# First weights in smaller pieces, x first on its queue, and the last output block in two halves

## The chip, the cores and the metric

The kernel runs on one core of one Trainium2 chip. The metric is the device time of one execution in microseconds (us); the time before is the median of three runs.

## The reference

One decoder block on x of 1024 tokens by 1024 channels, in float32:

```
xn   = rms_norm(x, norm1_g);  proj = xn @ w_in          # 1024 -> 5632 columns, cut into nine parts
q, k = rms_norm per head of 64;  v
A[t,s] = sigmoid(z_ts) * prod_{s<j<t} (1 - sigmoid(z_tj));  o_sb = A v      # 8 heads, strictly causal
HGRN2: f = lb + (1-lb) sigmoid(f_in);  S_t = diag(f_t) S_{t-1} + (1-f_t) i_t^T;  o_t = S_t^T silu(q_t)   # 4 heads
o_hg = rms_norm(o) * silu(g)
h    = x + (sigmoid(gate_sb) * (o_sb @ Wb1) + sigmoid(gate_hg) * (o_hg @ Wb2)) @ w_out
out  = h + (silu(rms_norm(h) @ w_gate) * (rms_norm(h) @ w_up)) @ w_down     # hidden 2816
```

## The kernel before

**Layout.** Everything is held transposed: channels on the 128 partitions, tokens along the free dimension, in two halves h of 512 tokens. A float32 product is made of three matmuls: every operand is split into a high part in the type fp32r and a low part (the operand less its high part, again fp32r), and high*high, high*low and low*high are summed in one PSUM bank of 128x512.

**Stage 1** multiplies x by the 44 column tiles of w_in (each 1024x128, brought in as a 128x1024 tile). `take_x(h)` (L528) loads the eight 128x512 blocks of x of a half, makes `ah` (xh: x times norm1_g, on ACT) and `al` (xl: the rest, on DVE), and squares each block on ACT for the norm; DVE adds the squares up in `tail`, one matmul sums them over the channels, and ACT turns the result into the factor `rr` (Ln, then Exp). The products are made from x without this factor; it is multiplied in by DVE when a bank is read (`aa<-pj,rr`, L587 on). `proj(ws, h)` (L565) makes the 24 matmuls of one column tile and one half of the tokens, k = 0 to 7 with three matmuls each; the first call makes the first two column tiles (q and k of the first pair of heads) side by side, 48 matmuls. Three PSUM banks of the name `pj` take these products, so that a fourth product waits until DVE has read one of the first three.

**The first loads.** The gains vector `vt` (128x27) is loaded first on SP's DMA queue (L236). The first half (k = 0 to 3) of the first two weight tiles, 128x512 or 256 KB each, is loaded on ACT's queue (L343 to L347); their second halves and x come on SP's queue in the order that `load` chains: x0, x1, x2, the second half of tile 0, x3, the second half of tile 1, x4 and so on. The first halves are split by ACT (the cast, `oh<-kb`) and DVE (the subtraction, `ol<-kb,oh`), the second halves by POOL and DVE (`split_w`, L517), as are all later weights of the stage. A short setup on DVE and ACT (L291 to L305) makes small vectors out of `vt`. Before its first product PE makes nine matmuls on a constant (`WARM`, L364).

**The order.** Stage 1 to the gate and up projections is written as a list of operations with costs, priorities (`rank`; higher goes first, equal ranks by the longest way to the stage's end) and buffer rings. `Plan.issue` (L131) runs this list through a model of the engines and issues the instructions in the order found there, all from L194. A buffer of a ring is free again for the planner when every operation that reads, writes or `holds` it is done. The order is fixed before the run: each engine executes its instructions in it and waits where an input is late.

**The end.** The down projection multiplies 512-column blocks p = 0 to 10; the last product keeps the last three p (`LAST`) for the end: for each of its four row blocks d it makes 9 matmuls of 512 columns into one PSUM bank (L1152), DVE adds the bank to `hb` (L1160), and SP's queue stores 256 KB to the output (L1162).

Of the kernel before, what the change touches and what calls it, by code (L numbers as in the profile page):

```python
# [10 lines left out]
F32 = mybir.dt.float32  # L11
# [4 lines left out]
ALU = mybir.AluOpType  # L16
# [12 lines left out]
LEVELS = [64, 32, 16, 8, 4, 2, 1]  # L29
FILL = ["GgGGaifq", "gGaGfiqGG", "gaGGGiqGfGG", "gGGG"]  # L30
BANKS = [3, 2, 3]
WARM = 9
ORDER = [1, 6, 2, 5, 7, 4, 3]
DOWN = [1, 6, 2, 7, 5, 4, 3]

# [179 lines left out]
def hybrid_block(ctx: ExitStack, tc, xT, wi, wb, wo, wg, wu, wd, vec, outT):  # L215
# [17 lines left out]
        return bank("ms", BANKS[2])  # L233

    vt = const.tile([P, V_W], F32, name="vt")
    nc.sync.dma_start(vt, vec)  # L236

    def load_w(src, pool=None):
        t = (pool or wpool).tile([P, 1024], F32, tag="w", bufs=2, name="w32")
# [70 lines left out]
    def hs(h):  # L310
        return slice(h * HALF, (h + 1) * HALF)
# [28 lines left out]
    st1 = ExitStack()  # L340
    hgp = st1.enter_context(tc.tile_pool(name="hgp", bufs=1, reuse_waits="tile"))

    first_w = []  # L343
    for n, v in fill_cols[:2]:
        t = hgp.tile([P, HALF], F32, tag="kb", bufs=4, name="kb")
        nc.scalar.dma_start(t, wi[COL[n] + v][:, :HALF])
        first_w.append(t)  # L347
    nc.scalar.preload_act_table_set("natural_log_exp_and_others")
    pre = ExitStack()
    pp = pre.enter_context(tc.tile_pool(name="prep", bufs=1))  # L350
# [78 lines left out]
    def new(ring, shape=(P, HALF), dt=F32):  # L429
        pool, cap, tag, phase = where[ring]  # L430
        plan.ring(ring, cap)

        def make():
            open_pools(phase)
            return (pools[pool] if phase else pool).tile(list(shape), dt, tag=tag, bufs=cap, name=tag)

        return Buf(ring, make, phase)
# [8 lines left out]
    def V(fn, *args, n=HALF, aps=0, rank=0, part=False, holds=(), after=(), **kw):  # L446
        cycles = 2 * n if fn == nc.vector.tensor_tensor_scan else n
        us = 0.067 + cycles / 960 + 0.061 * aps
        return plan.op("V", us, [(fn, args, kw)], rank, after, part=part, holds=holds)
# [37 lines left out]
    def pool_copy(dst, src, rank=0, after=(), holds=()):  # L487
        return G(nc.gpsimd.tensor_scalar, dst, src, 1.0, 0.0, op0=ALU.mult, op1=ALU.add, us=0.68,
                 rank=rank, after=after, holds=holds)
# [24 lines left out]
    def load(dst, src, kb, rank=1):  # L514
        last_load[0] = L(dst, src, kb, rank=rank, after=(last_load[0],))

    def split_w(src):  # L517
        hi, lo = new("oh", dt=F32R), new("ol", dt=F32R)
        last_split[0] = pool_copy(hi, src, rank=1, after=(last_split[0],))
        V(tt, lo, src, hi.bitcast(F32), op=ALU.subtract, rank=1)  # L520
        return hi, lo

    def take_w(col):
        w = new("w", (P, 1024))
        load(w, wi[col], 512)
        return [split_w(w[:, 512 * i:512 * i + 512]) for i in range(2)]

    def take_x(h):  # L528
        ss, acc, ws, sqs = new("ms"), new("tail"), [[], []], []
        if h == 0:  # L530
            plan.ring("kb", 4)
            for u in range(2):
                w = Buf("kb", lambda u=u: first_w[u])
                hi, lo = new("oh", dt=F32R), new("ol", dt=F32R)
                plan.at[A(nc.scalar.copy, hi, w, rank=3)] = 2.4 + 0.6 * u
                V(tt, lo, w, hi.bitcast(F32), op=ALU.subtract, rank=2)
                ws[u].append((hi, lo))
        for k in range(KT):
            x = new("aa" if h == 0 else ("xf", "xq", "xi", "xg")[k // 2])
            load(x, xT[k][:, hs(h)], 256)  # L540
            if h == 0 and k in (2, 3):
                u = k - 2
                n, v = fill[u]
                w = new("kb")
                load(w, wi[COL[n] + v][:, HALF:], 256)
                ws[u].append(split_w(w))
            g = vt[:, V_N1 + k:V_N1 + k + 1]
            A(act, xh[k][h][:, hs(h)], x, AF.Copy, scale=g, aps=1, rank=2 - h)
            V(stt, xl[k][h][:, hs(h)], x, g, xh[k][h][:, hs(h)].bitcast(F32), op0=ALU.mult,
              op1=ALU.subtract, aps=1, rank=2 - h)  # L550
            if k == 0:
                A(act, acc, x, AF.Square, rank=1 - h)
            else:
                sq = new("ww")
                A(act, sq, x, AF.Square, rank=1 - h)
                sqs.append(sq)
        for sq in sqs:
            V(tt, acc, acc, sq, op=ALU.add, rank=1 - h)
        M(2048, [(ss, ones, acc, True, True)])
        rstd(rr[h], ss, D, rank=1 - h)  # L560
        return ws
# [3 lines left out]
    def proj(ws, h, after=None):  # L565

        pss = [new("pj") for _ in ws]
        for k in range(KT):
            cols = slice(k % 4 * P, (k % 4 + 1) * P)
            for ps, w in zip(pss, ws):  # L570
                hi, lo = w[k // 4]
                last_fill[0] = M(1536, [
                    (ps, hi[:, cols], xh[k][h][:, hs(h)], k == 0, False),
                    (ps, hi[:, cols], xl[k][h][:, hs(h)], False, False),
                    (ps, lo[:, cols], xh[k][h][:, hs(h)], False, k == KT - 1)],
                    rank=-1, after=(last_fill[0], after))
            after = None
        return pss

# [600 lines left out]
            for d in range(4):  # L1180
                finish(o, d)
    rest = [(p, operands(o, p)) for p in range(NP - LAST, NP)]
    for d in range(4):
        for p, ops in rest:
            step(o, d, p, ops, False)
        finish(o, d)


def _layout(inputs):
# [45 lines left out]
```

## Time and profile before

| | us |
|---|---|
| median of 3 runs (lowest to highest) | 1520.84 (1519.15 to 1520.98) |
| the profiled execution's own time | 1520.8 |
| its span, first to last instruction | 1519.1 |
| PE busy | 1501.8 (99%) |
| DVE busy | 1194.1 (79%) |
| ACT busy | 804.3 (53%) |
| POOL busy | 110.3 (7%) |

A row of a list in order of time gives the start and the duration in us, the engine, the source line, the operation with output<-inputs, the number of merged instructions, and in brackets the engine's idle time before it with what ended it. Matmuls overlap: the row of one 128x512 matmul says 0.39 at TensorE's higher clock, while one starts every 0.226 to 0.23 us; so a pace is read from the differences of starts. In tables by windows each engine has its busy time and its count of instructions.

### The profile page before, as it was taken

How to read it: one execution, taken by the hardware profiler on the slowest of the kernel's cores; microseconds unless marked ns; L12 is line 12 of the kernel's file. 1: busy time of each engine (PE TensorE's matmuls, PEld its weight loads, DVE VectorE, ACT ScalarE, POOL GpSimd, SP SyncE). 2: the span in 40 equal slices, each digit the busy share in tenths (PEclk: the TensorE clock that was granted, in tenths of full speed). 3: DMA queues.
4: the chain of work that ended last, by engine and by line, in shares of the span. 5: the costliest groups of instructions: out<-in, count | busy, mean ns of one | idle time of the engine just before them, and what ended most of it. 6: DMA issues, size and time to landing. Idle time of an engine off the chain costs nothing.

```text
span 1519.1 us, 20504 instructions
## 1 busy us (share of the span) xinstructions
PE 1501.8 (99%) x7213; PEld 1238.3 (82%) x7213; DVE 1194.1 (79%) x2092; ACT 804.3 (53%) x1505; POOL 110.3 (7%) x155
## 2 busy tenths in 40 slices
PE   9999999999999999999999999999999999999999
PEld 6778888888888888888888888777888887888887
DVE  9898789988997877967867798788888888675553
ACT  7867779668758877445434453332332332354442
POOL 4210111211101100110000000000000000000000
PEclk9999999999999999999999999999999999999999
DMA  5111111111111212136434345444445544797662
GB/s 182 40 44 60 54 39 46 44 39 56 51 51 39 68 61 63 51 120 220 163 114 145 112 148 184 150 154 153 163 166 164 161 160 166 256 327 243 199 216 91
DMA packets 83159, 188.53 MB, mean 124 GB/s; under 512 B 9584, under 2 KB 11632, under 8 KB 83056
## 3 DMA queue, kind: packets, MB, share of 16 engines
q1 hardware_dynamic: 72400, 167.82, 34.2%
q10 hardware_dynamic: 10656, 19.40, 3.5%
q8 instruction: 57, 0.93, 0.3%
q14 instruction: 46, 0.38, 0.1%
HBM read 131.61 MB, written 55.57 MB: 123 GB/s over the span
## 4 chain that ended last, share of the span: by engine, by line
PE 69%; DVE 18%; DMA 5%; ACT 4%; issue 3%; POOL 1%; SPq 0%; DVEq 0%; ACTq 0%; POOLq 0%
PE pj L194 34%; PE f L1152 14%; PE ms L194 13%; PE z L194 8%; DVE ol L194 4%; DMA w<-wu 3%; DVE g L194 3%; DMA w<-wg 2%; DVE w L194 2%; DVE c L194 1%; DVE aa L194 1%; ACT aa L194 1%; ACT oh L194 1%; DVE kb L194 1%; DVE bs L194 1%
## 5 line engine op out<-in xcount | busy, mean ns | idle before, releaser
L194 PE MATMUL pj<-ah,oh 128*128 128x512 f32 x704 | 287.2, 408 | 2.4 <-ACT tmp L194 0.9
L194 PE MATMUL pj<-ah,ol 128*128 128x512 f32 x704 | 276.3, 393 | 0.0
L194 PE MATMUL pj<-al,oh 128*128 128x512 f32 x704 | 275.9, 392 | 0.0
L194 ACT CAST oh<-w 128x512 fp32r<-128x512 f32 x164 | 99.6, 619 | 237.3 <-DVE w L194 67.7
L194 DVE TENSOR_TENSOR ol<-w,oh 128x512 fp32r<-128x512 f32 x248 | 170.1, 686 | 31.0 <-ACT oh L194 23.5
L194 PE MATMUL ms<-f,oh 128*128 128x512 f32 x528 | 165.0, 394 | 3.1 <-DVE g L194 2.9
L194 PEld LDWEIGHTS pj<-ah,ol 128*128 128x128 f32 x704 | 132.6, 188 | 29.8
L194 PEld LDWEIGHTS pj<-ah,oh 128*128 128x128 f32 x704 | 132.9, 189 | 26.7 <-DVE aa L194 1.4
L194 PEld LDWEIGHTS pj<-al,oh 128*128 128x128 f32 x704 | 133.1, 189 | 23.1 <-DVE al L194 0.5
L194 PEld LDWEIGHTS ms<-f,oh 128*128 128x128 f32 x528 | 97.5, 188 | 29.5 <-DVE g L194 7.2
L1152 PE MATMUL f<-bh,ah 128*128 128x512 f32 x296 | 115.2, 389 | 0.0
L1152 PE MATMUL f<-bh,al 128*128 128x512 f32 x296 | 115.2, 389 | 0.0
L1152 PE MATMUL f<-bl,ah 128*128 128x512 f32 x296 | 115.1, 389 | 0.0
L194 DVE TENSOR_TENSOR_SCAN aa<-aa,ww 128x512 f32<-128x512 f32 (+3 forms) x96 | 94.2, 996 | 25.3 <-ACT aa L194 14.6
L194 PE MATMUL z<-f,oh 128*128 128x512 f32 x352 | 108.6, 390 | 0.0
L194 PE MATMUL pj<-f,oh 128*128 128x512 f32 x352 | 108.4, 389 | 0.0
L248 DVE TENSOR_TENSOR al<-ra,ah 128x512 fp32r<-128x512 f32 x73 | 50.4, 690 | 70.1 <-ACT ah L247 69.9
L194 PE MATMUL ms<-f,ol 128*128 128x512 f32 x264 | 102.9, 390 | 0.0
L194 POOL TENSOR_SCALAR oh<-w 128x512 fp32r<-128x512 f32 x84 | 68.4, 815 | 437.8 <-PE pj L194 367.7
L247 ACT CAST ah<-ra 128x512 fp32r<-128x512 f32 x73 | 45.5, 624 | 95.6 <-PE f L1152 83.8
L194 PE MATMUL pj<-mx,oh 128*128 128x512 f32 x256 | 78.7, 389 | 0.0
L194 PEld LDWEIGHTS pj<-f,oh 128*128 128x128 f32 x352 | 66.1, 188 | 13.7
(257 smaller groups left out, 3148.7 us busy)
## 6 DMA issues: line engine op xcount, KB each, us to landing
w<-wi SPq DMA_DIRECT2D x42, 512.0 KB, 3.6
rb<-act_d SPq DMA_DIRECT2D x73, 256.0 KB, 4.3
w<-wg SPq DMA_DIRECT2D x22, 512.0 KB, 4.3
w<-wu SPq DMA_DIRECT2D x22, 512.0 KB, 4.5
w<-wd SPq DMA_DIRECT2D x22, 512.0 KB, 5.0
wd_d<-ds SPq DMA_DIRECT2D x44, 256.0 KB, 2.8
ra<-wd_d SPq DMA_DIRECT2D x44, 256.0 KB, 4.1
act_d<-c SPq DMA_DIRECT2D x40, 256.0 KB, 4.2
```

The source lines that it names most:

```text
L194: fn(*[a.real() if isinstance(a, View) else a for a in args], **{k: v.real() if isinstance(v, View) else v for k, v in kw.items()})
L247: pin(nc.scalar.copy(hi, src))
L248: pin(nc.vector.tensor_tensor(lo, src, hi.bitcast(F32), op=ALU.subtract))
L1152: nc.tensor.matmul(banks[SET[o]][d], l[:, ws], r, start=start and i == 0, stop=p == NP - 1 and i == 2, skip_group_check=True)
```

## The change

`vt` leaves SP's queue, so that the first block of x is the first transfer there; ACT's queue now carries the first 128 KB of tile 0 (its k = 0 and 1), `vt`, and the first 128 KB of tile 1. The second 128 KB pieces (k = 2 and 3) are loaded on SP's queue after x1 and before x2. The first pieces are split by DVE alone (a cast of 256 columns and a subtraction of 256 columns each), the second pieces by ACT (the cast) and DVE. The ranks of these low parts are 3 and 2, and the second halves of the two tiles are split with rank 2. In every projection the matmul with the low weights goes second of the three, the one with the low x third; every matmul group of a projection holds the first piece of the first tile (`holds=w[0]`). `WARM` is 8. The last row block of the last product is made in two halves of 256 columns: 9 matmuls, an addition and a store for each half, the first on ACT's queue and the second on SP's.

```diff
-WARM = 9
+WARM = 8
     vt = const.tile([P, V_W], F32, name="vt")
-    nc.sync.dma_start(vt, vec)
-    first_w = []
-    for n, v in fill_cols[:2]:
-        t = hgp.tile([P, HALF], F32, tag="kb", bufs=4, name="kb")
-        nc.scalar.dma_start(t, wi[COL[n] + v][:, :HALF])
-        first_w.append(t)
+    first_w = [hgp.tile([P, HALF], F32, tag="kb", bufs=4, name="kb") for _ in range(2)]
+    first_w = [(t[:, :256], t[:, 256:]) for t in first_w]
+    first_src = [wi[COL[n] + v] for n, v in fill_cols[:2]]
+    nc.scalar.dma_start(first_w[0][0], first_src[0][:, :256])
+    nc.scalar.dma_start(vt, vec)
+    nc.scalar.dma_start(first_w[1][0], first_src[1][:, :256])
...
+    def first_piece(pieces, u, i):
+
+        cut, src = slice(256 * i, 256 * i + 256), fixed(first_w[u][i])
+        if i:
+            load(src, first_src[u][:, cut], 128)
+            hi, lo = (Buf(None, lambda b=b: b.buf.tile) for b in pieces[0])
+            op = A(nc.scalar.copy, hi[:, cut], src, n=256, rank=2, holds=pieces[0])
+        else:
+            hi, lo = new("oh", dt=F32R), new("ol", dt=F32R)
+            op = V(nc.vector.tensor_copy, hi[:, cut], src, n=256, rank=3)
+            plan.at[op] = 2.0 + 0.7 * u
+        V(tt, lo[:, cut], src, hi[:, cut].bitcast(F32), op=ALU.subtract, n=256, rank=3 - i)
+        pieces.append((hi, lo))
...
+            if h == 0 and k == 1:
+                for u in range(2):
+                    first_piece(ws[u], u, 1)
...
-                ws[u].append(split_w(w))
+                ws[u].append(split_w(w, 2))
...
-                hi, lo = w[k // 4]
+                hi, lo = w[k // 4 if len(w) == 2 else (0, 0, 1, 1, 2, 2, 2, 2)[k]]
                 last_fill[0] = M(1536, [
                     (ps, hi[:, cols], xh[k][h][:, hs(h)], k == 0, False),
-                    (ps, hi[:, cols], xl[k][h][:, hs(h)], False, False),
-                    (ps, lo[:, cols], xh[k][h][:, hs(h)], False, k == KT - 1)],
-                    rank=-1, after=(last_fill[0], after))
+                    (ps, lo[:, cols], xh[k][h][:, hs(h)], False, False),
+                    (ps, hi[:, cols], xl[k][h][:, hs(h)], False, k == KT - 1)],
+                    rank=-1, after=(last_fill[0], after), holds=w[0])
...
-    for d in range(4):
+    for d in range(3):
         for p, ops in rest:
             step(o, d, p, ops, False)
         finish(o, d)
+
+    k, h = TO[o][3]
+    t, ws = hb[k][:, hs(h)], slice(3 * P, 4 * P)
+    for c, queue in ((slice(0, 256), nc.scalar), (slice(256, 512), nc.sync)):
+        bank_ = banks[SET[o]][3][:, c]
+        for p, (hi, lo, bh, bl) in rest:
+            for i, (l, r) in enumerate(((hi, bh), (hi, bl), (lo, bh))):
+                nc.tensor.matmul(bank_, l[:, ws], r[:, c], start=False,
+                                 stop=p == NP - 1 and i == 2, skip_group_check=True)
+        nc.vector.tensor_tensor(t[:, c], bank_, t[:, c], op=ALU.add)
+        queue.dma_start(outT[k][:, hs(h)][:, c], t[:, c])
```

## Rows read from the trace of the kernel before

**Rows 1.** The page: the span, and busy time and share of the two busiest engines.

```profile
span 1519.1 us, 20504 instructions
...
PE 1501.8 (99%) x7213; PEld 1238.3 (82%) x7213; DVE 1194.1 (79%) x2092; ACT 804.3 (53%) x1505; POOL 110.3 (7%) x155
```

**Rows 2.** PE by windows: start and end of the window, its length, PE busy (instructions), granted clock, DMA share, GB/s.

```profile
0.00:38.00 38.00, 34.94 (x128) 1.00 0.52 182
38.00:456.00 418.00, 411.95 (x2239) 1.00 0.15 48
456.00:684.00 228.00, 227.71 (x1235) 1.00 0.21 67
```

**Rows 3.** What PE waited for over the whole span: us in total, times, longest.

```profile
PE ms L194 <- DVE g L194: 2.9, 5, 1.6
...
PE pj L194 <- DVE aa L194: 0.8, 1, 0.8
```

**Rows 4.** PE in order of time at the start: the nine constant matmuls, the first products, and the product that waits for a bank.

```profile
1.44 4.21 PE L365 MATMUL ms<-ones_r 128*128 128x512 f32 x9 [1.44 <-DVE ones_r L352]
...
6.31 0.80 PE L194 MATMUL pj<-ah,oh 128*128 128x512 f32 x1 [0.67 <-ACT ah L194]
...
7.10 0.79 PE L194 MATMUL pj<-al,oh 128*128 128x512 f32 x1
...
9.40 0.63 PE L194 MATMUL pj<-ah,oh 128*128 128x512 f32 x1
...
9.82 0.57 PE L194 MATMUL pj<-al,oh 128*128 128x512 f32 x1
...
10.46 0.40 PE L194 MATMUL pj<-ah,oh 128*128 128x512 f32 x1
...
10.70 0.39 PE L194 MATMUL pj<-al,oh 128*128 128x512 f32 x1
...
26.62 0.50 PE L194 MATMUL pj<-ah,oh 128*128 128x512 f32 x1 [0.78 <-DVE aa L194]
```

**Rows 5.** All engines by windows: length, then busy time and count of PE, PEld, DVE, ACT, POOL, then clock, DMA share and GB/s.

```profile
2.00:4.00 2.00, 2.00 (x6) 1.58 (x5) 0.46 (x4) 1.16 (x3) 1.78 (x2) 1.00 0.93 309
...
6.30:26.50 20.20, 19.53 (x74) 14.97 (x74) 20.20 (x32) 19.42 (x34) 8.69 (x16) 1.00 0.66 251
26.50:43.30 16.80, 16.49 (x66) 12.01 (x66) 16.71 (x27) 10.20 (x17) 7.18 (x12) 1.00 0.21 64
```

**Rows 6.** The first loads and their first users on ACT, in order of time; the second line is of the chain of waits (start, us, what).

```profile
0.80 0.89 ACTq L346 DMA_DIRECT2D kb<-wi  x2
0.80 0.39 SPq L236 DMA_DIRECT2D vt<-vec  x1
...
1.25 4.20 DMA aa<-xT
...
4.05 0.60 ACT L194 CAST oh<-kb 128x512 fp32r<-128x512 f32 x1
...
5.54 0.72 ACT L194 ACTIVATE ah<-aa,vt 128x512 fp32r<-128x512 f32 x1 [0.88 <-DMA aa<-xT]
```

**Rows 7.** DVE in order of time: the setup out of `vt`, the first subtractions, and the reading of the first bank with its neighbours.

```profile
3.39 0.15 DVE L291 TENSOR_SCALAR qg<-vt 128x1 f32<-128x1 f32 x1 [1.45 <-DMA vt<-vec]
...
4.18 0.16 DVE L301 TENSOR_TENSOR e<-e,e 128x4 f32<-128x4 f32 x1 [0.30 <-ACT e L300]
...
4.87 0.69 DVE L194 TENSOR_TENSOR ol<-kb,oh 128x512 fp32r<-128x512 f32 x1
...
6.29 0.75 DVE L194 SCALAR_TENSOR_TENSOR al<-aa,vt,ah 128x512 fp32r<-128x512 f32 x1 [0.65 <-ACT ah L194]
...
24.68 0.68 DVE L194 TENSOR_TENSOR ol<-w,oh 128x512 fp32r<-128x512 f32 x1
...
25.89 0.68 DVE L194 TENSOR_TENSOR aa<-pj,rr 128x512 f32<-128x512 f32 x1
```

**Rows 8.** DVE's operations of 256 columns (two subtractions merged in one row, 0.61 us for both).

```profile
55.47 0.61 DVE L194 TENSOR_TENSOR ww<-z,aa 128x256 f32<-128x256 f32 x2
```

**Rows 9.** The end, in order of time.

```profile
1513.22 0.39 PE L1152 MATMUL f<-bh,ah 128*128 128x512 f32 x1
...
1515.03 0.39 PE L1152 MATMUL f<-bh,al 128*128 128x512 f32 x1
1515.46 0.69 DVE L1160 TENSOR_TENSOR hb<-f,hb 128x512 f32<-128x512 f32 x1 [1.35 <-PE f L1152]
1516.18 0.33 SPq L1162 DMA_DIRECT2D outT<-hb  x1
```

**Rows 10.** Stores: size and median us from issue to landing.

```profile
o_d<-ot SPq DMA_DIRECT2D x32, 64.0 KB, 1.9
o_d<-tail SPq DMA_DIRECT2D x8, 256.0 KB, 2.0
```

**Rows 11.** Consecutive matmuls of 256 columns on PE.

```profile
109.71 0.28 PE L194 MATMUL ms<-th,vv 128*128 128x256 f32 x1
109.83 0.28 PE L194 MATMUL ms<-tl,vv 128*128 128x256 f32 x1
```

**Rows 12.** POOL's splits of the two halves of a later weight tile; each waits for the matmul that frees its buffer.

```profile
57.58 0.62 POOL L194 TENSOR_SCALAR oh<-w 128x512 fp32r<-128x512 f32 x1 [9.32 <-PE pj L194]
60.67 0.62 POOL L194 TENSOR_SCALAR oh<-w 128x512 fp32r<-128x512 f32 x1 [2.47 <-PE pj L194]
```

More of the change, by code (lines that the diff above doesn't have):

```diff
@@ L515, in load, with split_w @@
         last_load[0] = L(dst, src, kb, rank=rank, after=(last_load[0],))
-    def split_w(src):
+    def split_w(src, rank=1):
         hi, lo = new("oh", dt=F32R), new("ol", dt=F32R)
-        last_split[0] = pool_copy(hi, src, rank=1, after=(last_split[0],))
-        V(tt, lo, src, hi.bitcast(F32), op=ALU.subtract, rank=1)
+        last_split[0] = pool_copy(hi, src, rank=rank, after=(last_split[0],))
+        V(tt, lo, src, hi.bitcast(F32), op=ALU.subtract, rank=rank)
         return hi, lo
@@ L530, in take_x @@
         if h == 0:
-            plan.ring("kb", 4)
             for u in range(2):
[L533 to L537, printed above, removed]
+                first_piece(ws[u], u, 0)
         for k in range(KT):
```

## The prediction

> **What bounds the kernel now.** I read the page first: PE is busy for 1501.8 of 1519.1 us [rows 1], so only its idle or slow time can be won, 17 us at most. The windows say where that lies: 3.1 us before 38 us, 6.1 us between 38 and 456 us, 0.3 us from there to 684 us [rows 2]. The list of PE's waits holds small sums only [rows 3]. The change touches the two ends, so I read both in order of time.
>
> At the start PE runs nine constant matmuls until 5.65 us, idles 0.67 us until the first high x is made, and makes its first product at 6.31 us. The second comes 0.79 us later, where two of the following ones are 0.42 us apart (9.40, 9.82): it waited some 0.37 us for the low x. From about 10.2 us matmuls come 0.24 us apart (10.46, 10.70), so TensorE went from 1.2 to 2.4 GHz there. At 26.62 us PE has waited 0.78 us for a bank which DVE reads from 25.89 us on [rows 4, 7]. And DVE is without a gap: busy 20.20 of 20.20 us from 6.30 to 26.50 us and 16.71 of 16.80 us up to 43.30 us [rows 5]. So in the first 43 us PE's small stalls are DVE's lateness: what PE wins ahead of 26.62 us turns into a longer wait there unless DVE also comes earlier. That is the reading on which the forecast rests.
>
> **The loads.** x0 is issued at 1.25 us behind `vt`, and lands 4.20 us later, at 5.45 us [rows 6]. First on its queue it is issued 0.45 us earlier. In front of or beside it ACT's queue then has 269 KB in place of 512 KB; the 243 KB less are 0.79 us at the 309 GB/s of the window from 2 to 4 us [rows 5], of which x0 can gain between nothing and all; I take half, 0.40 us. So x0 lands at 4.6 us (4.2 to 5.0). ACT makes `ah` from 0.09 us after the landing and PE starts 0.77 us after ACT [rows 4, 6], were it not for ACT's two small Exps, which wait for DVE's first setup steps out of `vt`. `vt` goes out second on ACT's queue, where two issues take 0.89 us [rows 6], so 0.45 us later: it lands at 3.84 in place of 3.39 us [rows 7], or at 4.3 us if the pieces slow it as much again. DVE's step after the Exps came 0.79 us after the first step on `vt` [rows 7], so ACT is free at 4.6 to 5.1 us. First product: about 4.75 + 0.77 = 5.5 us, 0.8 us earlier. The constant matmuls, now eight, stop 0.47 us sooner (4.21/9) at 5.2 us and are in nobody's way. With the low weights second, the low x has 0.84 us at the pace of 0.42 us, and its DVE instruction lasts 0.75 us [rows 7]: the stall of 0.37 us goes if DVE is free. The matmuls are otherwise the same in number and size, so their order costs nothing.
>
> **DVE pays for it.** ACT's two casts of 512 columns become two of 256 on ACT and two on DVE, and the low parts of the first halves become four subtractions of 256 columns. Two operations of 256 columns took 0.61 us [rows 8], so 0.31 us each; 512 columns come 0.60 us apart (24.68 to 25.89, two operations [rows 7]). DVE's added work is 2 x 0.31 + 4 x 0.31 - 2 x 0.60 = 0.66 us. It had 0.30 and 0.65 us of gaps ahead of its stream [rows 7]. Before the first low x it has to do: the setup, 1.48 us from 3.39 to 4.87 us less the 0.30 us gap that can be filled, and one more small step (0.16 us, like its neighbours [rows 7]); and four operations of 256 columns, 1.24 us. From 3.84 us that ends at 6.4 us; if the first piece's two operations are done before `vt` lands, at 5.8 us. The second is nearer: the whole 256 KB piece was there at 4.05 us without a wait [rows 6], and half of it comes sooner. So the stream starts at 5.9 us in place of 6.29 us; behind it two subtractions of 256 columns stand where one of 512 stood (0.62 against 0.60 us), so DVE is 0.4 us earlier from there on (0.5 earlier to 0.1 later).
>
> **The order around the read.** The planner now holds the first piece of the first tile to the end of its 24 matmuls for the second half of the tokens, so the split of the third weight tile, whose subtraction stands at 24.68 us right ahead of the bank's read, may fall behind it: 0 or 0.60 us earlier for the read [rows 7]. I take 0.3. Sum of the start: -0.7 us. PE itself would be 0.8 + 0.37 = 1.2 us earlier if the clock rises as long after the first product as now, and 0.5 us if it rises at 10.2 us all the same (4.7 us at 0.42 us are 11.2 products in place of nine, 2.2 x 0.24); either way nearly the 0.7 us, and the rest becomes wait at the bank.
>
> **The later order.** Each of the 42 later weight tiles is held as well: the first half's buffer is now counted free with the second, 3.1 us later in the row's example [rows 12]. A tile's 48 matmuls are 11 us of PE, so the next split has time, and I cost it at nothing; but every order in the 418 us up to 456 us can come out differently, with 6.1 us of idle PE in it [rows 2]. I take 0 within 1.2 us.
>
> **The end.** Now the block's 9 matmuls start from 1513.22 to 1515.03 us, DVE adds at 1515.46 us for 0.69 us, and the store is issued at 1516.18 us [rows 9]. Halves: matmuls of 256 columns come 0.12 us apart and last 0.28 us [rows 11], 18 x 0.12 = 2.16 against 9 x 0.226 = 2.03 us. If nothing stops PE between the halves, the last one starts at 1513.22 + 17 x 0.12 = 1515.26 us and ends at 1515.54 us; DVE lasts 0.69 less half of 0.60, so 0.4 us; the store goes out at 1516.0 us, 0.2 us earlier. But the two halves lie in one bank, and DVE's addition of the first stands between them. In the waits PE stands for DVE when it writes on in a bank that DVE has just read [rows 3]; no row shows different columns of one. If PE waits: the first half ends at 1514.46, DVE is done at 1514.9, PE's last matmul starts 0.05 + 0.96 us later and ends at 1516.2, and the store goes out at 1516.65 us, 0.45 us later than now. Stores of 64 and of 256 KB land in 1.9 and 2.0 us [rows 10], so half the size gives 0.05 us. I take the wait: +0.4 us (bounds -0.25 and +0.45).
>
> The Trainium skill (PSUM — Partial Sum Buffer, "PSUM bank collisions raise a hardware error") says that semaphores should guard PSUM by bank and quadrant and not by address, since an engine that reads any columns of a bank while TensorE writes others collides. By that rule the end costs 0.4 us; by guarding the columns alone it would give 0.25 us. No row here decides it.
>
> **Sum.** -0.7 + 0.4 = -0.3 us against the profiled execution's own 1520.8 us (span 1519.1 plus 1.7 around it), which is the median within 0.04 us: 1520.5 us. About 0.2% (3 us) is what a measurement of this kernel can tell from no change.
>
> **Rivals.**
> - *The halves overlap* (columns guarded, not the bank): -0.7 - 0.25, 1519.9 us. 15%.
> - *PE keeps what it wins.* The first 43 us are PE's after all, because the planner takes low-ranked work out of DVE's way. The most is 0.8 + 0.37 us and nine products at 0.42 made at 0.24 us (1.6 us), 2.8 us; against it speaks DVE without a gap [rows 5]; for it, that only one bank stall stands in the list [rows 3]. With two thirds of it, -1.9 + 0.4: 1519.3 us; it decides where DVE's read comes before 25 us. 18%.
>  The Trainium skill (TensorE: Matmul & The Clock Gate, Part 1, The HAM clock gate) says that the array starts throttled and sustained activity releases it; by that the closed gap would bring the rise forward, and this rival is where it would pay.
> - *DVE is late (slower).* `vt` lands at 4.3 us and the pieces not before it: 4.3 + 1.48 - 0.30 + 0.16 + 1.24 = 6.9 us for the first low x, 0.6 us later than now, and nothing moves at the read. +0.6 + 0.4: 1521.8 us. It decides from a start of the stream after 6.29 us. 12%.
> - *PE runs out of split weights.* The held buffers make splits late: a quarter of the 42 tiles at the 0.3 us of a typical short wait is 3 us: 1523.5 us. The 11 us of cover speak against it. 5%.
>
> My forecast has 50%, its own range 1519.3 to 1521.7 us by the 1.2 us of the order. Eight in ten over all: 1518.5 to 1522.2 us. Faster by over 0.2% needs the second rival nearly whole or much luck in the order: 9%. Slower by over 0.2%: the last rival and the tail, 5%. Within 0.2%: 86%.
>
> **What the profile would show.** Right: the first product at 5.0 to 6.0 us with the low x close behind; DVE without a gap from about 5.9 to 43 us; a wait of PE for `aa` near 26 us at least as long as 0.78 us; at the end a gap of PE of some 0.5 us between the halves, and the last store issued 0.4 us later after the first of these matmuls than now. Wrong: no bank wait near 26 us while PE is over 1.5 us ahead; new waits of `pj` for `ol` or `oh`; PE's idle time between 38 and 456 us far from 6.1 us, which would make the order, and not the edit's own steps, the cause.

## The result and the profile after

The changed kernel takes 1523.15 us (median of 22 runs, 1519.96 to 1526.86) beside 1519.78 us for the kernel before (22 runs, 1517.13 to 1523.57): ratio 1.0024 [1.0016, 1.0031], 3.4 us slower and outside the forecast range.

The page of the changed kernel, against [rows 1]. PE is busy 1.8 us less and idle 2.6 us more, and 0.8 us of span is all that one profiled execution shows:

```profile
span 1519.9 us, 20493 instructions
...
PE 1500.0 (99%) x7221; PEld 1238.4 (81%) x7221; DVE 1197.2 (79%) x2097; ACT 802.7 (53%) x1505; POOL 114.3 (8%) x155
```

The span hides the loss. The gate and up projections, which the change doesn't touch, took 431.2 us from their first matmul to the first of the down projection in the profile of before, 429.4 in a second profile of the same kernel (e4 below) and 428.5 in this one; two profiles of one kernel differ here by 1.8 us, over half of the loss. So I compare fixed points of the program. The first product of the branch projection, which ends stage 1, starts at 700.49 us before and at 703.56 after, 3.07 us later; from the first matmul of the last row block to the end of the span it is 5.85 us before (1513.22 to 1519.07) and 6.36 after (1513.58 to 1519.94). The two sum to 3.6 us, close to the 3.4 that the runs show.

Two more fixed points say where in stage 1 the 3.07 us are lost. Counted in PE's list without the constants, both kernels have made the same matmuls, by their names, up to the 75th (the one that waited for the bank in [rows 4]) and up to the 81st ahead of the branch. PE in order of time, these two and the branch, first in the kernel before, then in the changed one; the 75th of before is in [rows 4], at 26.62 us:

```profile
682.13 0.39 PE L194 MATMUL pj<-ah,oh 128*128 128x512 f32 x1
...
700.49 0.62 PE L194 MATMUL pj<-o,oh 128*128 128x512 f32 x2
```

```profile
27.10 0.50 PE L194 MATMUL pj<-ah,oh 128*128 128x512 f32 x1
...
683.05 0.39 PE L194 MATMUL pj<-ah,oh 128*128 128x512 f32 x1
...
703.56 0.62 PE L194 MATMUL pj<-o,oh 128*128 128x512 f32 x2
```

The changed kernel is 0.48 us late at the 75th matmul, 0.92 us at the second point and 3.07 us at the branch. So 2.15 us, most of the loss, arise in the last 20 us of stage 1.

PE by windows of the changed kernel, columns as in [rows 2], with one more stretch up to just before the branch of the kernel before:

```profile
0.00:38.00 38.00, 33.59 (x124) 0.96 0.54 181
38.00:456.00 418.00, 412.93 (x2232) 1.00 0.16 48
456.00:684.00 228.00, 226.57 (x1238) 1.00 0.20 61
684.00:700.00 16.00, 14.19 (x63) 1.00 1.00 356
```

Length less busy time is PE's idle time: 4.41, 5.07, 1.43 and 1.81 us, where before had 3.06, 6.05, 0.29 and 0.00. The differences, +1.35, -0.98, +1.14 and +1.81, sum to 3.32 us, about the loss of stage 1: three stretches idle more and one less. The stretches are of time and not of work, so a single one is no cost by itself: of the first one's 1.35 us, 0.66 are the constant matmul that is gone (the nine took 4.21 us, the eight 3.55). The list of PE's waits (total, times, longest), against [rows 3]:

```profile
PE ms L194 <- DVE g L194: 3.1, 6, 1.2
...
PE ms L194 <- DVE tl L194: 2.1, 5, 1.3
PE pj L194 <- ACT ah L194: 2.0, 1, 2.0
PE pj L194 <- DVE ol L194: 1.8, 1, 1.8
...
PE pj L194 <- DVE al L194: 0.7, 1, 0.7
PE f L1206 <- DVE hb L1208: 0.5, 1, 0.5
```

Five single waits stand out: `ah` and `al` at the start, `tl` at 44 us (1.27 us, for the low part of the squares of a norm), `ol` late in stage 1, `hb` at the end.

**The start.** All engines in order of time, against [rows 4, 6, 7]:

```profile
1.25 0.45 ACTq L346 DMA_DIRECT2D vt<-vec  x1
...
4.66 0.33 SPq L194 DMA_DIRECT2D kb<-wi  x1
4.67 0.29 DVE L194 CAST oh<-kb 128x256 fp32r<-128x256 f32 x1 [2.72 <-DMA kb<-wi]
...
6.09 0.33 SPq L194 DMA_DIRECT2D kb<-wi  x1
6.10 0.15 DVE L290 TENSOR_SCALAR qg<-vt 128x1 f32<-128x1 f32 x1 [0.68 <-DMA vt<-vec]
6.16 0.72 ACT L194 ACTIVATE ah<-aa,vt 128x512 fp32r<-128x512 f32 x1 [2.67 <-DMA vt<-vec]
...
6.94 0.50 PE L194 MATMUL pj<-ah,oh 128*128 128x512 f32 x1 [1.95 <-ACT ah L194]
...
7.54 0.74 DVE L194 SCALAR_TENSOR_TENSOR al<-aa,vt,ah 128x512 fp32r<-128x512 f32 x1
...
8.34 0.79 PE L194 MATMUL pj<-al,oh 128*128 128x512 f32 x1 [0.66 <-DVE al L194]
```

`vt`, 13.5 KB, is issued at 1.25 us and used at 6.10, 4.85 us later; ahead of the pieces it took 2.6 (0.80 to 3.39 [rows 6, 7]). ACT has been idle 2.67 us when it comes, and PE stands 1.95 us. The first low x is begun at 7.54 us, before at 6.29. PE by short windows, columns as in [rows 2] (the granted clock stands behind the count of instructions):

```profile
5.00:7.00 2.00, 0.06 (x1) 1.00 1.04 332
7.00:8.00 1.00, 0.67 (x2) 1.00 0.90 258
8.00:11.00 3.00, 2.67 (x6) 0.50 0.87 242
11.00:12.00 1.00, 1.00 (x5) 0.79 0.99 371
```

After the idle stretch the clock falls from 2.4 to 1.2 GHz at 8 us and is back only past 11 us. Against before this is hardly a second loss: there the first eight products ran at the pace of 1.2 GHz too, up to 10.2 us [rows 4]. (The granted clock says 1.00 for before all this while [rows 5]; there the starts tell the pace.) The tenth product starts at 11.46 us, before at 10.46; of this 1.0 us the later first product is 0.63 us and the longer wait for the low x (0.66 us, before some 0.37) the rest.

**The seam.** Why PE waits for `ol` at 695 us, in order of time (all engines):

```profile
678.36 0.33 SPq L194 DMA_DIRECT2D o_d<-tail  x1
678.79 11.52 SPq L194 DMA_DIRECT2D ld<-o_d  x8
...
688.06 0.62 POOL L194 TENSOR_SCALAR oh<-w 128x512 fp32r<-128x512 f32 x1 [10.26 <-PE pj L194]
688.74 2.44 DVE L194 TENSOR_TENSOR o<-ld,o 128x1024 fp32r<-128x1024 f32 x2 [0.67 <-ACT o L194]
...
692.49 1.05 ACT L194 CAST o<-ld 128x1024 fp32r<-128x1024 f32 x1 [2.56 <-DMA ld<-o_d]
...
693.57 1.23 DVE L194 TENSOR_TENSOR o<-ld,o 128x1024 fp32r<-128x1024 f32 x1 [2.39 <-ACT o L194]
...
694.71 1.29 DVE L194 TENSOR_TENSOR ol<-w,oh 128x512 fp32r<-128x512 f32 x2
...
695.45 0.50 PE L194 MATMUL pj<-ah,ol 128*128 128x512 f32 x1 [1.81 <-DVE ol L194]
```

POOL had made the high part of the last gate tile at 688.7 us. DVE could have subtracted then, but it runs in the planner's order, and that order puts six subtractions `o<-ld` of the next stage first. They work on what ACT makes of the loads, 512 KB each. The eight loads stand in one row on SP's queue, 1.4 us apart, with the DMA engines full (share 1.00 in the window above). So DVE idles 2.39 us for work that nobody needs yet, and PE idles behind it. Before, the last store ahead of these loads was issued at 674.20 us, 4.2 us earlier, five of the loads went out in a row in place of eight, and the subtraction stood behind five of the others, the last of them begun at 688.23 us, early enough for PE (SP and DVE of the kernel before, in order of time):

```profile
674.20 0.33 SPq L194 DMA_DIRECT2D o_d<-tail  x1
674.62 7.45 SPq L194 DMA_DIRECT2D ld<-o_d  x5
...
688.23 1.22 DVE L194 TENSOR_TENSOR o<-ld,o 128x1024 fp32r<-128x1024 f32 x1 [2.50 <-ACT o L194]
...
690.58 0.68 DVE L194 TENSOR_TENSOR ol<-w,oh 128x512 fp32r<-128x512 f32 x1
```

**The end**, against [rows 9]:

```profile
1513.58 0.28 PE L1206 MATMUL f<-bh,ah 128*128 128x256 f32 x1
...
1514.85 0.42 DVE L1208 TENSOR_TENSOR hb<-f,hb 128x256 f32<-128x256 f32 x1 [0.38 <-PE f L1206]
...
1515.33 0.39 PE L1206 MATMUL f<-bh,ah 128*128 128x256 f32 x1 [0.52 <-DVE hb L1208]
...
1516.70 0.42 DVE L1208 TENSOR_TENSOR hb<-f,hb 128x256 f32<-128x256 f32 x1 [1.42 <-PE f L1206]
...
1517.15 0.33 SPq L1209 DMA_DIRECT2D outT<-hb  x1
```

The second half starts when DVE has read the first. The last store is issued 3.57 us after the block's first matmul, before 2.96 us.

### The profile page after: what moved, and what is told of

It reads as the page before. It is cut to its first block, busy times and chain, and to the rows that moved or that the text cites. A ratio compares the mean times of both kernels' runs of the same rounds, so it can differ in the third digit from the quotient of the medians.

```text
span 1519.9 us, 20493 instructions
## 1 busy us (share of the span) xinstructions
PE 1500.0 (99%) x7221; PEld 1238.4 (81%) x7221; DVE 1197.2 (79%) x2097; ACT 802.7 (53%) x1505; POOL 114.3 (8%) x155
## 4 chain that ended last, share of the span: by engine, by line
PE 73%; DVE 17%; ACT 4%; DMA 3%; issue 2%; POOL 1%; SPq 0%; ACTq 0%; DVEq 0%; POOLq 0%
PE pj L194 32%; PE ms L194 17%; PE f L1164 14%; PE z L194 10%; DVE ol L194 3%; DVE aa L194 2%; ACT aa L194 2%; DVE kb L194 1%; DVE tl L194 1%; DMA w<-wu 1%; DVE g L194 1%; DVE tail L194 1%; DMA w<-wg 1%; DVE dl L194 1%; DVE w L194 1%
```

## The experiments

All were timed against the kernel before. The expectations use these names. BANK: the halves at the end wait because they share one PSUM bank. QUEUE: `vt` is late because of its place behind a piece on ACT's queue. START: the late start is carried to the end of stage 1. HOLD: the held buffers cost the time in the later order. SEAM: the wait for `ol` at the end of stage 1 comes from DVE's queue, by loads that the planner takes for faster than they are. LOTTERY: any change of the planner's input draws another order with other waits.

The ratio, and from every profile the start of the first product, PE's idle time by stretch (us, from the windows), the start of the 81st matmul ahead of the branch and that of the first branch product:

| run | ratio to before | first product | 0-38 | 38-456 | 456-684 | 684-700 | 81st ahead | branch |
|---|---|---|---|---|---|---|---|---|
| before | 1 | 6.31 | 3.06 | 6.05 | 0.29 | 0.00 | 682.13 | 700.49 |
| after | 1.0024 [1.0016, 1.0031] | 6.94 | 4.41 | 5.07 | 1.43 | 1.81 | 683.05 | 703.56 |
| e1 | 1.0020 [1.0009, 1.0031] | 7.23 | 4.60 | 5.06 | 1.41 | 2.32 | 683.44 | 704.46 |
| e2 | 1.0014 [1.0002, 1.0026] | 5.48 | 2.79 | 4.90 | 1.17 | 2.77 | 681.03 | 702.49 |
| e3 | 1.0004 [0.9992, 1.0016] | 6.44 | 2.63 | 4.93 | 1.03 | 2.23 | 681.04 | 701.92 |
| e4 | 1.0008 [0.9998, 1.0018] | 6.23 | 3.11 | 6.19 | 0.29 | 0.00 | 682.57 | 700.93 |
| e5 | 1.0058 [1.0043, 1.0073] | 6.93 | 3.91 | 5.66 | 2.38 | 2.18 | 685.44 | 706.32 |
| e6 | 1.0027 [1.0016, 1.0038] | 6.40 | 3.63 | 4.90 | 1.38 | 2.82 | 682.79 | 705.83 |
| e7 | 1.0004 [0.9995, 1.0012] | 5.82 | 4.19 | 6.16 | 0.29 | 0.00 | 682.31 | 700.67 |
| e8 | 1.0055 [1.0041, 1.0069] | 5.97 | 3.88 | 5.40 | 2.30 | 1.95 | 683.75 | 704.35 |
| e9 | 1.0001 [0.9990, 1.0012] | 7.04 | 4.02 | 4.69 | 1.38 | 0.00 | 682.67 | 701.03 |
| e10 | 1.0003 [0.9992, 1.0014] | 7.68 | 5.26 | 6.11 | 0.28 | 0.00 | 684.12 | 702.48 |
| e11 | 0.9994 [0.9982, 1.0006] | 7.25 | 6.10 | 4.40 | 0.89 | 0.18 | 682.55 | 701.39 |
| e12 | 0.9992 [0.9980, 1.0004] | 5.73 | 2.54 | 4.94 | 1.18 | 0.00 | 681.37 | 699.73 |

The last two columns tell the seam from all that is ahead of it. From the one to the other it is 18.36 us in the six profiles without a wait there (before, e4, e7, e9, e10, e12), 18.84 in e11, which waits 0.18 us, and 20.51 to 23.04 in the seven that wait 1.8 us or more.

**e4, the kernel before once more.** No edit.

> The kernel before once more, for what one execution's trace can tell: if stage 1 is settled by the order and the loads, its first branch matmul lies within 0.5 us of 700.49 us again, while the gate and up stage (874.6 to 1300.5 us in the first trace, 425.9 us long, against 423.3 us in the changed kernel's) is free to differ by 2 to 3 us; if instead stage 1 itself scatters by 2 us or more, the 3.07 us between the two traces say little.

It gave 1.0008 [0.9998, 1.0018]: a ratio within 0.1% of 1 tells nothing. The table's idle times repeat to 0.14 us in every stretch and the branch to 0.44 us, so they tell far more than the totals. Other profiles set limits to this: e7 has the same stage 1, idles 1.13 us more before 38 us and yet reaches the branch within 0.2 us, and e1, with the stage 1 of the changed kernel, reaches it 0.90 us later than that.

**e1, the end undone.** In the changed kernel the last row block is whole again:

```diff
-    for d in range(3):
+    for d in range(4):
...
-    for c, queue in ((slice(0, 256), nc.scalar), (slice(256, 512), nc.sync)):
...
-        queue.dma_start(outT[k][:, hs(h)][:, c], t[:, c])
```

> The changed kernel with its last row block whole again (one bank, 9 matmuls of 512 columns, one store). If the halves cost what the traces show (last store issued 3.57 us after the block's first matmul against 2.96 us before, and its landing 0.17 us shorter), the store goes out 2.96 us after the block's first matmul again and the kernel gains 0.4 to 0.5 us on the changed one; all theories share this. Everything ahead of the end stays: first product near 6.9 us, first matmul of the branch products (pj<-oo) near 703.5 us. Whoever holds the end for the main loss expects the time of before, ratio 1.000; whoever holds stage 1 for it expects 1.0018 to 1.0024.

The last store is again 2.96 us after the block's first matmul, and yet the kernel stays at 1.0020: the end is the small part. (The branch, expected near 703.5 us, starts at 704.46.)

**e2, `vt` back on SP's queue.** The changed kernel with

```diff
+    nc.sync.dma_start(vt, vec)
     nc.scalar.dma_start(first_w[0][0], first_src[0][:, :256])
-    nc.scalar.dma_start(vt, vec)
```

> The changed kernel with the gains vector first on SP's queue again, x behind it; the planner's order is the same as in the changed kernel. Theory START (the late vector costs the time): the first product comes at 5.2 to 6.0 us instead of 6.94 us, stage 1 ends 1 to 3 us earlier (first branch matmul at 700.5 to 702.5 us) and the ratio to before falls to 1.0005 to 1.0015. Theory ORDER (the planner's changed order of stage 1 costs it): the first product comes as early, but the first branch matmul stays within 0.5 us of 703.56 us, the 1.81 us wait of PE for a low part near 695 us stays, and the ratio is that of the changed kernel, 1.002.

`vt` lands 2.0 us after its issue, and the first product comes at 5.48 us although x0 is second on its queue. The first stretch has 1.62 us less idle time; ahead of the seam PE is 2.0 us earlier than in the changed kernel and 1.1 us earlier than before. The wait at the seam is 0.96 us longer, so the branch starts only 1.07 us earlier. Both theories are right in part: START for the time and the ratio, ORDER for the wait that stays.

**e3, the hold alone.** The kernel before with

```diff
-                    rank=-1, after=(last_fill[0], after))
+                    rank=-1, after=(last_fill[0], after), holds=w[0])
```

> The kernel before with one edit: every matmul group of a projection holds the first piece of its first tile (holds=w[0]), which changes the planner's order and nothing else. ORDER with the hold as its cause: the first branch matmul moves from 700.5 us to 702 to 704 us and the ratio is 1.001 to 1.002. START: the order of stage 1 makes no difference beyond 0.5 us, 700.0 to 701.0 us and a ratio of 1.000.

One argument, which changes the order of the instructions alone, brings the wait at the seam (2.23 us), 0.7 us more idle time from 456 to 684 us and 1.1 us less from 38 to 456: the pattern of the changed kernel. (`w` is the group's own tile, so each tile's own first piece is held.) Ahead of the seam this order is a gain: PE is there 1.1 us earlier than before, and the branch starts 1.43 us later all the same, a little short of the 702 us expected. The ratio can't be told from 1.

**e5, all but the hold.** The changed kernel with

```diff
-                    rank=-1, after=(last_fill[0], after), holds=w[0])
+                    rank=-1, after=(last_fill[0], after), holds=w[0] if len(w) == 3 else ())
```

> The changed kernel with the hold only where it is needed (holds=w[0] in the groups of the first two tiles alone, whose pieces share one buffer). Theory HOLD (holding the first piece in all later tiles makes the planner put the last gate tile's split behind the loads of the next part on DVE): PE's wait for a low part near 695 us, 1.8 to 2.8 us in every trace with the hold, is gone or under 0.3 us, the first branch matmul comes 1 to 2.5 us earlier than in the changed kernel (701.0 to 702.5 us), ratio to before 1.0005 to 1.0015. Rival (any change of the order does it, the hold has no special part): the wait near 695 us stays, and the branch products start at 703 to 704.5 us. The first product stays late, 6.9 to 7.3 us.

HOLD falls. The wait at the seam stays (2.18 us), idle time from 456 to 684 us grows to 2.38 us, and at 1.0058 it is the slowest of all; the branch, at 706.32 us, is later than the rival expected too, and a wait of 2.68 us at 970 us follows behind it. The wait at the seam doesn't need the hold: with the hold and without it the planner draws an order that has it.

**e6, `vt` first on ACT's queue.** The changed kernel with

```diff
+    nc.scalar.dma_start(vt, vec)
     nc.scalar.dma_start(first_w[0][0], first_src[0][:, :256])
-    nc.scalar.dma_start(vt, vec)
```

> The changed kernel with the gains vector first on ACT's queue, ahead of both pieces; x stays first on SP's. Theory QUEUE (the vector was late because it stood behind a 128 KB piece on its queue): it lands at 2.8 to 3.5 us as it did first on SP's queue, the first product comes at 4.8 to 5.6 us, and stage 1 ends like that of the kernel with the vector on SP's queue (702.5 us) or up to 0.6 us earlier. Rival (its 128 small rows are slow on ACT's queue wherever they stand, or beside x): it lands after 4 us again, and the first product comes after 6 us. The wait near 695 us stays in both, since the planner's order is that of the changed kernel.

QUEUE holds: on the same queue, but first, `vt` lands 2.8 us after its issue. The expected 4.8 to 5.6 us for the first product were missed all the same: the first piece is now the late one (first product at 6.40 us, after 1.18 us of waiting for `oh`). The seam cost more here, and the branch misses its forecast of some 702.5 us too. PE by windows:

```profile
692.00:695.00 3.00, 1.38 (x7) 1.00 1.02 403
695.00:696.00 1.00, 0.00 (x0) 1.00 1.04 422
696.00:699.50 3.50, 3.30 (x8) 0.52 0.88 304
699.50:702.00 2.50, 2.50 (x13) 0.99 1.01 360
```

After the wait of 2.82 us for `ol` the clock is at 1.2 GHz for 3.5 us; the branch starts at 705.83 us.

**e7, the halves in two banks.** The kernel before with the last block in halves, the second in another bank, whose earlier sum DVE adds to `hb` beforehand:

```diff
+    nc.vector.tensor_tensor(t[:, high], banks[0][3][:, high], t[:, high], op=ALU.add)
...
+    for c, bank_, new_, queue in ((low, banks[0][3][:, low], False, nc.scalar),
+                                  (high, banks[1][3][:, low], True, nc.sync)):
```

> The kernel before with one edit at the end: the last row block in two halves of 256 columns, the second half in a bank of its own (its earlier sum is added by DVE beforehand). Theory BANK (the 0.5 us gap between the halves is PE's wait for DVE's reading of the same bank): no gap between the halves, the last store goes out 2.7 to 2.85 us after the block's first matmul (before 2.96 us, with both halves in one bank 3.57 us), and the span from that matmul to the end is 5.5 to 5.75 us (before 5.85 us, changed 6.36 us). Rival (the gap has another cause, such as the start of a new column range): the gap stays, and the store goes out at about 3.5 us. Of the total this is 0.2 us at most, a ratio of 1.000.

BANK holds. PE and SP of this kernel, in order of time:

```profile
1511.33 0.28 PE L1196 MATMUL f<-bh,ah 128*128 128x256 f32 x1
...
1512.28 0.28 PE L1196 MATMUL f<-bh,al 128*128 128x256 f32 x1
1512.40 0.28 PE L1196 MATMUL f<-bh,ah 128*128 128x256 f32 x1
...
1514.13 0.33 SPq L1200 DMA_DIRECT2D outT<-hb  x1
```

The second half follows 0.12 us behind the first. The store goes out after 2.80 us, against 2.96 and 3.57; to the end of the span it is 5.42 us, a little under the 5.5 expected. The total can't show 0.4 us.

This profile also tells of the start, which is that of before. By chance PE reached the pace of 2.4 GHz at 6.9 us and made its products ahead of time. It won nothing:

```profile
26.63 0.50 PE L194 MATMUL pj<-ah,oh 128*128 128x512 f32 x1 [0.93 <-DVE aa L194]
```

In [rows 4] the same product started at 26.62 us after a wait of 0.78.

**e8, three parts undone.** The changed kernel with the edits of e1, e2 and e5 together.

> The changed kernel with its three suspected costs taken out together: the gains vector first on SP's queue, the hold only in the first two tiles, the last block whole. What stays are the 128 KB pieces split by DVE, the low weights second, the ranks and eight warm-up matmuls. If HOLD, the late vector and the halves are the whole loss, the first product comes near 5.5 us, no wait of over 0.3 us stands near 695 us, the branch products start at 699.5 to 701 us and the ratio to before is 0.999 to 1.0005. If the other order changes of stage 1 cost as well, the branch products start at 702 us or later and the ratio stays above 1.001.

At 1.0055 it is as slow as e5. With the start mended and the end whole, the idle time of stage 1 lies in the order: 2.30 us from 456 to 684 and 1.95 at the seam. The branch is 3.86 us late; the ratio stands for some 8 us, and where the rest is lost was not traced.

**e9, the planner told of slow loads.** The changed kernel with

```diff
-        L(t, od[k], 512)
+        L(t, od[k], 512, land=6.0)
```

> The changed kernel with one number of the planner's model corrected: the eight loads of o_d (512 KB each) count as landed after 6.0 us, their median in the trace, instead of 2.0 us. The order on PE and POOL is the changed kernel's; DVE and ACT change only around the end of stage 1. Theory SEAM (near 695 us the last gate tile's low part stands on DVE behind six subtractions for the next part, which wait for those loads): DVE makes the low part before the fifth of them, PE's wait of 1.8 to 2.8 us is gone or under 0.5 us, the first branch matmul comes 1.5 to 3 us after the changed kernel's order would allow it, that is at 701 to 702.5 us with a first product near 7 us, and the ratio falls from 1.0024 to 1.0005 to 1.0015. Rival (PE only loses the time a little later, since the branch products then wait for the same loads): the wait near 695 us goes, but a wait of the same size appears at the first branch matmuls and they start no earlier than 703 us.

SEAM holds. The planner's model had the loads land after 2 us; in the profile of the changed kernel their median is 5.8. Told of 6, it leaves PE's and POOL's orders in stage 1 as they were, sends four loads in a row in place of eight, and puts three subtractions of the next stage ahead of the one that PE needs in place of six. DVE in order of time, from the last of the three:

```profile
690.88 1.21 DVE L194 TENSOR_TENSOR o<-ld,o 128x1024 fp32r<-128x1024 f32 x1
692.02 0.68 DVE L194 TENSOR_TENSOR ol<-w,oh 128x512 fp32r<-128x512 f32 x1
692.62 1.22 DVE L194 TENSOR_TENSOR o<-ld,o 128x1024 fp32r<-128x1024 f32 x1
```

The wait is gone and the branch starts 2.53 us earlier than in the changed kernel: 0.38 us ahead of the seam, and 2.15 at the seam, all that the seam had cost against before. The ratio is 1.0001, under the 1.0005 expected. The start is as late as ever (7.04 us).

**e10, `vt` behind a piece in the kernel before.** The planned order is untouched:

```diff
-    nc.sync.dma_start(vt, vec)
...
+        if not first_w:
+            nc.scalar.dma_start(vt, vec)
```

> The kernel before with one edit: the gains vector is loaded second on ACT's queue, between the two 256 KB first pieces, and x first on SP's. The planner's order is untouched. Theory START (that queue place alone makes the vector late, and the late start is carried to the end of stage 1): the vector lands after 5.5 us (3.39 us before), the first product comes at 6.9 to 8 us, and the branch products start 0.5 to 2 us later than 700.5 to 700.9 us. Rival (the late start is absorbed by DVE's queue in the first 45 us): the first product is as late, but the branch products start within 0.4 us of 700.9 us.

`vt` takes 5.0 us here too, the first product comes at 7.68 us, and the product that waits for the bank at 28.33 instead of 26.62. The branch starts 1.99 us later (1.55 against e4): START holds, and nothing absorbs it on the way. The total doesn't show it (1.0003, with an interval up to 1.0014).

**e11, a small change of the planner's input.** The kernel before with the first casts planned 0.4 and 0.3 us earlier:

```diff
-                plan.at[A(nc.scalar.copy, hi, w, rank=3)] = 2.4 + 0.6 * u
+                plan.at[A(nc.scalar.copy, hi, w, rank=3)] = 2.0 + 0.7 * u
```

> The kernel before with a change of no weight: ACT's casts of the two first pieces are allowed to the planner from 2.0 and 2.7 us of its clock instead of 2.4 and 3.0 us. No work, load or priority changes; the planner's order of stage 1 comes out differently. Theory LOTTERY (the order of before is a favourable one of many, and any change of the list draws another): the sums of PE's waits differ in many places, the branch products start 1 us or more later than 700.5 to 700.9 us, and a wait of PE for a low part near the end of stage 1 of over 1 us appears in it too. Rival (it takes the particular edits of this change to lose time): the branch products start within 0.5 us of 700.7 us and no such wait appears.

LOTTERY is not shown, nor is its rival. The order changes and idle time moves by over a microsecond in two stretches, but at the seam it is 0.18 us, and the branch starts 0.7 us behind the middle of the two profiles of before, between the two forecasts: not every order has that wait.

**e12, mended.** The changed kernel with the edits of e2 and e9, and the end of e7.

> The changed kernel mended where the traces put its loss: the gains vector first on SP's queue, the loads of o_d counted at 6.0 us by the planner, the second half of the last row block in a bank of its own. If SEAM, START and BANK are the loss, the first product comes near 5.5 us, no wait of over 0.5 us stands near 695 us, the branch products start at 699 to 700.5 us, the last store goes out 2.8 us after its block's first matmul, and the ratio is 0.998 to 0.9998. If the order costs elsewhere, the branch products start after 701 us and the ratio stays at 1.000 or above.

First product 5.73 us, no wait at the seam, the last store after 2.80 us, branch at 699.73 us, the earliest of all. Ahead of the seam it is 0.77 us earlier than before, and still so at the branch. 1518.08 us is the lowest median of this study; 0.9992 [0.9980, 1.0004] is not clear of the kernel before.

## Why the prediction was wrong, and where it was right

**Failed: "The later order ... I cost it at nothing ... I take 0 within 1.2 us."** From the 75th matmul to the branch the changed kernel falls 2.59 us behind, outside those bounds: 0.44 us up to the seam and 2.15 us there. The forecast looked for the cost at the held buffers, weighed the time to make a split ("11 us of PE"), and set the bound from the 6.1 us of idle PE up to 456 us. Up to the seam the bound held, though a new wait of 1.27 us for `tl` at 44 us is in it. The cost came at a place with no idle PE at all before (0.00 us): a stage without waits has nothing to give and much to lose. The rival *PE runs out of split weights* had the sign, the size (3 us) and the kind of wait (`pj` for `ol`, which the forecast names as a sign of being wrong), at 5%, but by luck, for the mechanism was another: the split weights did run out, once, but the high part was ready 6 us earlier, the wait stayed without the hold (e5), and DVE's queue stood behind transfers (e9). What was not read is the seam between two stages, where DVE's and SP's work for the next stage mixes with the last of this one.

**Failed: "it lands at 3.84 ... or at 4.3 us if the pieces slow it as much again".** `vt` landed at 6.10 us. The step shifted the old landing by the 0.45 us of the later issue; [rows 6] had no small transfer behind a large one on a queue, and I set its bound by one more such step. e6 and e10 show that being second on the queue is the cause: 2.8 us first, 5.0 second. Whether it is the piece in front or the issue 0.45 us later, with the DMA engines filling up, they don't separate. That is the rival *DVE is late*, given 12% and +0.6; it came at +1.25 us for the first low x, and the start, forecast at -0.7 us, stood at +0.48 at the 75th matmul. With `vt` in time it stood at -0.87 (e2, 25.75 us) and -0.65 (e12, 25.97 us), close to the forecast, though with `vt` first and x0 second, another order of the loads than the forecast's. The landing of x0, forecast for 4.6 us (4.2 to 5.0), hides behind `vt` in the changed kernel; in e6, with x0 first on its queue, ACT uses it at 4.30 us without a wait. "Half of it comes sooner" failed beside x0: the first piece was used at 4.67 us, where the whole was there at 4.05; with `vt` first on SP's queue it was there by 3.11 us (e2).

**Right: DVE sets the first 43 us.** Not by the sign that was named (in the changed kernel PE was the later one near 26 us and that wait vanished), but e7 shows it: PE's faster products changed nothing at 26.63 us. A late `vt` makes DVE late as well (busy 18.93 of 18.96 us from 7.54 to 26.50), and e10 carries that to the end of stage 1: the first product is 1.37 us late there, the branch 1.99. So a loss at the start is kept where a gain of PE's alone is not. The order around the bank's read helped as forecast or more (0.3, 0 to 0.6): the split of the third tile fell behind the read, and DVE began the read at 26.36 us, 0.47 us later than before, though the first low x was 1.25 us late. The hold alone does it (e3: the 75th matmul at 26.27 us, 0.35 earlier, behind a first product 0.13 later). This gain hides part of what `vt` cost.

**Right: the end.** Forecast +0.4 (gap 0.5 us, store 0.45 us later); the gap was 0.52 us, the store 0.61 us later after the block's first matmul, and +0.51 us to the end of the span, 0.1 beyond the term. The Trainium skill (PSUM — Partial Sum Buffer, "PSUM bank collisions raise a hardware error") asks for guarding PSUM by bank and not by address. The trace shows this kernel guarded so, with a wait of 0.52 us between halves that share no column and none in two banks (e7); no run left the guard out. *The halves overlap* falls.

**The clock.** The forecast let it rise at the latest where it had. It was up at the first product and fell again, to 1.2 GHz for 3 us, behind the 1.95 us of idle PE; the products that started at its pace were seven in place of eight, so this is no cost against before. The Trainium skill (TensorE: Matmul & The Clock Gate, Part 1, The HAM clock gate) says that sustained activity releases the throttle; the trace agrees in that direction, with the fall behind 1.95 us without a matmul and the rise behind seven products. When it rises is not settled by the kernel alone: with the loads and the order of before the pace of 2.4 GHz came at 10.2, 10.9 and 6.9 us (before, e4, e7).

Added up, at points of equal work: the start gave +0.48 us in place of -0.7, the order +2.59 in place of 0, the end +0.51 in place of +0.4, together 3.6 us in place of -0.3. Open is why just these edits draw orders with the wait at the seam: all profiles with eight loads in a row have it (after, e1, e2, e3, e5, e6, e8), of those with five or four only e11 waits, 0.18 us, and e10, which issues the store ahead of them at 676.22 us like e3, has five and no wait. Which of the planner's choices put the eight in a row was not traced. How often that wait also drops the clock, as in one profile of seven, is open too.

## What to carry to other kernels

Where a program orders fixed queues by a model, an edit of its input can be an edit of the whole order (here the hold was, and the two start times of e11; the load time of e9 was not): read the seams between stages before costing such an edit at nothing, above all those that have no idle time to lose, and give the model the load times of the trace. An in-order engine that serves two stages must not have the next stage's DMA-bound work in front of what the busiest engine needs now. And when runs scatter by more than the effect, compare fixed points of equal work, such as the start of the same matmul; idle time in a stretch of time can move without any loss.

## What the hardware showed unexpectedly

- 13.5 KB second on a queue behind a piece of 128 or 256 KB took 4.8 to 5.0 us to land (after, e10); first on its queue 2.0 to 2.8 us (e2, e6, before).
- What was first on SP's queue told for the first piece on ACT's. Beside the 13.5 KB of `vt` 256 KB were there by 4.05 us (before) and 128 KB by 3.11 and 3.26 (e2, e12); beside the 256 KB of x0 the 256 KB were used at 4.99 us (e10) and the 128 KB at 4.67 and 4.43 (after, e9), with DVE or ACT waiting. The forecast let x0 gain and the piece lose nothing.
- SP's queue paused between issues: its loads of second pieces went out at 4.66 and 6.09 us in the changed kernel, the moments at which a first piece and `vt` landed. Why it waits for them no run shows.
- Waits of 1.95 to 2.48 us at the start (after, e1, e10, e11), of 2.68 us at 970 us (e5) and of 2.82 us at the seam (e6) were followed by 1.2 GHz for some 3 us, while waits of 1.8 to 2.8 us at the seam in other profiles (after, e1, e2, e3) were not.
